# Six loads in two transfers each, in a prefix log-sum-exp on one core

## The chip, the cores and the metric

The kernel runs on one core of one Trainium2 chip. The metric is the device time in microseconds (us), smaller is better; it is given as the median of several runs. A profile of one execution stands beside it: its span runs from the first to the last instruction of that execution.

## What is computed

The input x has the shape (4, 4096, 4128): four batches, 4096 time steps, 4128 columns, all float32. The output is the running log-sum-exp along the time steps:

```python
out[:, 0, :] = x[:, 0, :]
for t in range(1, S):
    mx = np.maximum(out[:, t - 1, :], x[:, t, :])
    out[:, t, :] = mx + np.log(np.exp(out[:, t - 1, :] - mx) + np.exp(x[:, t, :] - mx))
```

So out[t] is the logarithm of the sum of exp(x) over all steps up to t. Input and output have 270.5 MB each.

## The kernel before, in words

**Tiles.** The kernel takes exp of all values, forms running sums and takes their logarithm. One step of the kernel handles 128 x r consecutive time steps of one batch, with r = 2 or 3: partition p of the tile (a row of SBUF, the on-chip memory) holds r neighbouring time steps of 4128 columns each. A load or a store of such a tile is one transfer of 128 rows with 16,512 bytes times r per row: 33,024 bytes for r = 2 (4,128 KB in all) and 49,536 bytes for r = 3 (6,192 KB). The lists `begin`, `usual` and `final` (L149 to L151) give r for each step of a batch; the first batch starts with 2, 2, 2, 3, 2, 3. There are 49 steps, 49 loads and 49 stores.

**Slots.** Four slots in SBUF hold the tiles in turn (x0 to x3; L71 and L72). A load may go into a slot once the store of the step four before it is done.

**One step.** Each tile is cut into three chunks of 1376 columns. For each chunk ScalarE (ACT) takes exp in place (L102); VectorE (DVE) adds up the r time steps of a partition (L114, L116) into a vector z; TensorE (PE) multiplies z by a triangular matrix (L124), which gives each partition the sum of all partitions before it and the carry of the step before; VectorE adds that to the tile (L133) and forms the last time step's sum in z (L141, or L136 in a batch's last step); ScalarE takes the logarithms (L146, L147).

**Order.** The order on each engine is written out by hand in lists (L166 to L205), and a loop (L220 to L233) emits the operations once their inputs have been emitted. All transfers are issued by SyncE (SP) on one queue. The list `moves` (L166 to L175) sets their order: loads 0 to 3, store 0, store 1, load 4, store 2, load 5, store 3, load 6 and so on. SP takes this list in order: a store waits on SP for the logarithms of its step, and a load waits on SP for the store that frees its slot, with everything after them held back.

**Completion.** Each transfer counts up one of eight semaphores, which the framework gives out in turn. At the kernel's end SP waits for each of these in turn, and a check on the inputs' range (L236 to L256) decides whether a slow general routine must run; it does not for this input.

The change is in `Step.load` (L87 and L88), which issues one transfer for a tile, and ahead of `begin` (L149).

Of the kernel before, what the change touches and what calls it, by code (L numbers as in the profile page):

```python
# [12 lines left out]
P = 128  # L13
# [8 lines left out]
def kernel(  # L22
# [5 lines left out]
    nc = tc.nc  # L28
# [17 lines left out]
        out=below, in_=below, pattern=[[1, P]], compare_op=ALU.is_ge,  # L46
# [5 lines left out]
        out=carried, in_=below, pattern=[[0, P]], compare_op=ALU.not_equal,  # L52
# [25 lines left out]
    class Step:  # L78
# [6 lines left out]
            return rows.rearrange("(p j) d -> p j d", j=self.r)  # L85

        def load(self):  # L87
            nc.sync.dma_start(out=self.xt, in_=self.dram(x))  # L88

        def store(self):  # L90
            nc.sync.dma_start(out=self.dram(out), in_=self.xt)  # L91
# [1 line left out]
    class Chunk:  # L93
# [49 lines left out]
        def log(self):  # L143
            t, r = self.t, self.t.r
            e = t.xt[:, 0:r - 1, self.cols]
            nc.scalar.activation(e, e, ACT.Ln)  # L146
            nc.scalar.activation(t.xt[:, r - 1, self.cols], self.z, ACT.Ln)  # L147

    begin = [2, 2, 2, 3, 2, 3, 2, 3, 2, 3, 3, 3, 2]  # L149
    usual = [3, 2, 3, 2, 3, 3, 3, 2, 3, 3, 3, 2]  # L150
# [70 lines left out]
    while any(at[e] < len(l) for e, l in lists.items()):  # L221
# [17 lines left out]
        out=fits[:, :B * NC], in0=probe, scalar1=LARGE, scalar2=None, op0=ALU.is_le,  # L239
    )  # L240
    nc.vector.tensor_scalar(
        out=fits[0:1, B * NC:], in0=short, scalar1=0.0, scalar2=None, op0=ALU.is_le,
# [7 lines left out]
        out=flag, in0=good, scalar1=float(P), scalar2=None, op0=ALU.is_lt,  # L250
# [62 lines left out]
```

## Time and profile before

| | before |
|---|---|
| median of 3 runs | 1260.83 us (1260.6 to 1261.09) |
| span of the profiled execution | 1258.4 us |
| DVE busy | 956.2 us (76%), 548 instructions |
| ACT busy | 955.4 us (76%), 466 instructions |
| PE busy | 602.4 us (48%), 884 instructions |
| moved by DMA | 541.28 MB, mean 430 GB/s |
| packets of all transfers of the kernel (queue q1) | 14,112, of which 1,568 of 4 bytes |
| load of 6,192 KB: issue to landing | 38.4 us median, 30 of them |
| load of 4,128 KB | 33.0 us median, 19 of them |
| store of 6,192 KB and of 4,128 KB | 25.0 us and 21.6 us median |

The profile gives no time of the execution other than its span; the median of the timed runs is 2.4 us longer. How to read it: the page has a busy share for each engine, then 40 equal slices of the span with a digit for each engine (tenths busy) and the rate of the DMA in GB/s. "DMA share" is the mean busy share of the core's 16 DMA engines, which together work off what SP puts on its queue. A table by stage gives the same for stretches of time that the reader chooses: length, then for each engine busy time and (in brackets) instructions, then the granted TensorE clock, the DMA share and the GB/s. SPq is SP's issuing of transfers. Single records of the trace hold a start and a length for each row of a transfer and for the 4-byte records that end a transfer, 16 for each.

### The profile page before, as it was taken

To read this page: it belongs to the slowest core of one execution; us is meant where nothing else is said; L and a number is where in the kernel's file an instruction comes from. 1 tells how busy PE (TensorE), PEld (TensorE's weight loads), DVE (VectorE), ACT (ScalarE), POOL (GpSimd) and SP (SyncE) were. 2 spreads that over 40 slices of the span, in tenths; PEclk is the share of its full clock that TensorE was granted. 3 is DMA by queue.
4 is the path that set the end of the run, shared out by engine and by line. 5 is a ranking of instruction groups with operands and counts; after the bars stand their busy time and mean duration, and the time that the engine had idled before them with its cause. 6 is when DMAs were issued, how large, how long until landed. Compare 5 with 4: busy or idle time off the path is not lost.

```text
span 1258.4 us, 3228 instructions
## 1 busy us (share of the span) xinstructions
PE 602.4 (48%) x884; PEld 233.1 (19%) x884; DVE 956.2 (76%) x548; ACT 955.4 (76%) x466; POOL 4.6 (0%) x14
## 2 busy tenths in 40 slices
PE   3654454453535455345364535634535553463361
PEld 1221121121212122112121212211211211121120
DVE  3997696795967699579596679957957976795792
ACT  6987687786976699578697668866968966896792
POOL 1000000000000000000000000000000000000000
PEclk9877776676677667666676666766766776676676
DMA  9999999999999999999999999999999999999998
GB/s 403 420 439 426 432 436 428 432 437 429 439 425 438 430 437 433 436 435 427 440 422 436 436 432 434 434 430 435 437 428 437 431 435 431 434 437 433 432 435 354
DMA packets 14131, 541.28 MB, mean 430 GB/s; under 512 B 1568, under 2 KB 1568, under 8 KB 1568
## 3 DMA queue, kind: packets, MB, share of 16 engines
q1 hardware_dynamic: 14112, 541.07, 99.6%
q8 instruction: 7, 0.11, 0.0%
q14 instruction: 12, 0.10, 0.0%
HBM read 270.53 MB, written 270.53 MB: 430 GB/s over the span
## 4 chain that ended last, share of the span: by engine, by line
DMA 69%; ACT 14%; DVE 13%; PE 1%; issue 1%; SPq 0%; ACTq 0%; DVEq 0%
DMA x<-in_x_dram 52%; DMA out_dram<-x 17%; ACT x L102 6%; DVE x L133 5%; ACT x L146 5%; DVE z L116 3%; ACT x L147 3%; DVE z L141 3%; DVE x L114 2%; PE p L124 1%; SPq L91 0%; DVE z L136 0%; ACTq L146 0%; ACTq L254 0%; SPq L88 0%
## 5 line engine op out<-in xcount | busy, mean ns | idle before, releaser
L124 PE MATMUL p<-z,carried 128*128 128x512 f32 (+1 forms) x810 | 551.8, 842 | 544.3 <-DVE z L116 544.3
L102 ACT ACTIVATE x<-x 128x4128 f32<-128x4128 f32 (+1 forms) x147 | 468.0, 3187 | 219.7 <-DMA x<-in_x_dram 219.7
L124 PEld LDWEIGHTS p<-z,carried 128*128 128x128 f32 x810 | 213.4, 280 | 882.2 <-DVE z L116 648.3
L133 DVE TENSOR_TENSOR x<-p,x 128x2752 f32<-128x2752 f32 (+1 forms) x147 | 361.9, 2462 | 6.2 <-PE p L124 6.2
L146 ACT ACTIVATE x<-x 128x2752 f32<-128x2752 f32 (+1 forms) x147 | 300.6, 2045 | 63.5 <-DVE z L141 58.5
L114 DVE TENSOR_TENSOR x<-x 128x1376 f32<-128x1376 f32 x90 | 142.9, 1588 | 216.5 <-ACT x L102 216.5
L116 DVE TENSOR_TENSOR z<-x 127x1376 f32<-127x1376 f32 x147 | 233.9, 1591 | 53.8 <-ACT x L102 49.4
L141 DVE TENSOR_TENSOR z<-x 128x1376 f32<-128x1376 f32 x135 | 215.0, 1592 | 4.6
L147 ACT ACTIVATE x<-z 128x1376 f32<-128x1376 f32 x147 | 196.0, 1334 | 0.0
L124 PE MATMUL p<-z,below 128*128 128x512 f32 (+1 forms) x72 | 50.4, 864 | 87.4 <-DVE z L116 87.4
L124 PEld LDWEIGHTS p<-z,below 128*128 128x128 f32 x72 | 19.6, 289 | 117.7 <-DVE z L116 78.8
L136 DVE CUSTOM_DVE_ANT_0 z<-x 128x1376 f32<-128x1376 f32 x12 | 19.1, 1592 | 0.4
L105 ACT ACTIVATE spare<-x,tiny 1x1376 f32<-1x1376 f32 x12 | 17.3, 1442 | 0.5
L69 POOL MEMSET z<- 128x1376 f32 x3 | 3.7, 1241 | 0.0
L105 ACT ACTIVATION_READ_ACCUMULATOR spare<-x,tiny 1x1 f32 x12 | 2.2, 186 | 0.0
L247 PE MATMUL good<-ones,low 128*1 128x1 f32 x2 | 0.2, 164 | 3.8 <-DVE low L245 3.8
L34 ACT ACT_TABLE_LOAD x1 | 1.3, 1283 | 0.8 <-PEq L297 0.8
L136 DVE DVE_READ_ACCUMULATOR2_ANT probe<- 128x1 f32 x12 | 1.0, 83 | 0.0
L247 PEld LDWEIGHTS good<-ones,low 128*1 128x1 f32 x2 | 0.1, 80 | 4.8 <-DVE low L245 4.8
L249 DVE TENSOR_SCALAR flag<-good 1x1 int32<-1x1 f32 x1 | 0.1, 148 | 0.3 <-PE good L247 0.3
L51 POOL TENSOR_SCALAR_AFFINE_SELECT carried<-below 128x128 f32<-128x128 f32 x1 | 0.3, 290 | 0.0
L45 POOL TENSOR_SCALAR_AFFINE_SELECT below<-below 128x128 f32<-128x128 f32 x1 | 0.3, 285 | 0.0
(13 smaller groups left out, 1.6 us busy)
## 6 DMA issues: line engine op xcount, KB each, us to landing
x<-in_x_dram SPq DMA_DIRECT2D x30, 6192.0 KB, 38.4
out_dram<-x SPq DMA_DIRECT2D x30, 6192.0 KB, 25.0
x<-in_x_dram SPq DMA_DIRECT2D x19, 4128.0 KB, 33.0
out_dram<-x SPq DMA_DIRECT2D x19, 4128.0 KB, 21.6
```

The lines of the kernel that those rows point to most:

```text
L34: nc.scalar.preload_act_table_set("natural_log_exp_and_others")
L69: nc.gpsimd.memset(t, 0.0)
L102: nc.scalar.activation(e, e, ACT.Exp)
L105: nc.scalar.activation(spare, t.xt[0:1, 0, self.cols], ACT.Relu, bias=tiny, scale=-1.0, accum_out=short[:, k:k + 1],)
L114: nc.vector.tensor_tensor(out=e[1], in0=e[0], in1=e[1], op=ALU.add)
L116: nc.vector.tensor_tensor(out=self.z[0:n], in0=e[r - 2][0:n], in1=e[r - 1][0:n], op=ALU.add,)
L124: nc.tensor.matmul(pt[:, a:b], lhsT=w, rhs=self.z[:, a:b], start=True, stop=True,)
L133: nc.vector.tensor_tensor(out=e, in0=base, in1=e, op=ALU.add)
L136: nc.vector.tensor_tensor_reduce(out=self.z, in0=ends[0], in1=ends[1], scale=1.0, scalar=0.0, op0=ALU.add, op1=ALU.add, accum_out=probe[:, ...
L141: nc.vector.tensor_tensor(out=self.z, in0=ends[0], in1=ends[1], op=ALU.add)
L146: nc.scalar.activation(e, e, ACT.Ln)
L147: nc.scalar.activation(t.xt[:, r - 1, self.cols], self.z, ACT.Ln)
```

## The change

`load` issues one transfer for each part of a list of partition ranges, and the list has two entries for steps 0 to 5 and one for all others. Step 0 goes out as partitions 0 to 15 and 16 to 127, steps 1 to 5 as partitions 0 to 63 and 64 to 127. Both parts stand one behind the other on SP. The run then has 104 transfers in place of 98.

```diff
         def load(self):
-            nc.sync.dma_start(out=self.xt, in_=self.dram(x))
+            for a, b in parts.get(self.n, [(0, P)]):
+                nc.sync.dma_start(out=self.xt[a:b], in_=self.dram(x)[a:b])
...
+    parts = {0: [(0, 16), (16, P)]}
+    parts.update((k, [(0, P // 2), (P // 2, P)]) for k in range(1, 6))
+
     begin = [2, 2, 2, 3, 2, 3, 2, 3, 2, 3, 3, 3, 2]
```

## The prediction

> **What bounds the kernel now.** I read the slices of the page first, then the DMA queues, then the table by stage, and only then the engines.
>
> ```profile
> DVE  3997696795967699579596679957957976795792
> ACT  6987687786976699578697668866968966896792
> ...
> DMA  9999999999999999999999999999999999999998
> GB/s 403 420 439 426 432 436 428 432 437 429 439 425 438 430 437 433 436 435 427 440 422 436 436 432 434 434 430 435 437 428 437 431 435 431 434 437 433 432 435 354
> ```
> ```profile
> q1 hardware_dynamic: 14112, 541.07, 99.6%
> ```
>
> See that no engine is at its limit for long, while the 16 DMA engines are busy in every slice and move 420 to 440 GB/s in every slice but the first and the last. 541.07 MB at 433 GB/s is 1250 us of a span of 1258.4. So the end is set by the DMA queue's own work, all of it on one queue (q1, issued by SP), and a microsecond lost there is lost at the end: no compute wait can give it back. The trace's records agree: summed over the 16 engines, they are idle for only 5.8 us of the span, 2.1 of it at the start, 3.1 at the end (the engines run dry between 1251 and 1257 us), and 0.6 in all the rest.
>
> The second question is what sets the pace of a busy DMA engine. This is the table by stage, with the DMA share and GB/s as its last columns:
>
> ```profile
> 15.00:20.00 5.00, 2.60 (x3) 1.17 (x4) 1.90 (x2) 4.87 (x5) 0.00 (x0) 1.00 1.01 436
> 20.00:25.00 5.00, 4.62 (x10) 1.99 (x8) 3.90 (x3) 4.97 (x5) 0.00 (x0) 1.00 1.01 436
> ...
> 1245.00:1250.00 5.00, 0.00 (x0) 0.00 (x0) 0.00 (x0) 0.00 (x0) 0.00 (x0) 0.50 1.01 436
> 1250.00:1255.00 5.00, 0.00 (x0) 0.00 (x0) 0.00 (x0) 0.00 (x0) 0.00 (x0) 0.50 0.56 239
> ```
>
> At 15 to 25 us only loads are in flight; at 1245 to 1255 only stores. Both run at 436 GB/s. And when half of the engines have run dry (share 0.56), the rate falls in proportion: 239 / 0.56 = 427. The engines that are left do not get faster, so the pace is no shared total; it is private to each of the 16 paths. Single records say the same: a row of 33,024 bytes takes 1.222 us in all but 3% of 4,864 cases, one of 49,536 bytes 1.829 us, both 27 GB/s, 1/16 of 436. Private to what, though: to the DMA engine, or to the group of SBUF rows at its other end? In this kernel every transfer has all 128 rows, so that the two are never seen apart. The change pulls them apart, and everything hangs on that.
>
> **The change, part by part.** It changes `load` (L87-L88) for steps 0 to 5. Six transfers are added; no byte, no compute instruction, no order of loads and stores on SP.
>
> 1. Issue. In the profile the first four loads are issued back to back from 0.80 us:
>
> ```profile
> 0.80 1.91 SPq L88 DMA_DIRECT2D x<-in_x_dram  x4
> 38.04 15.04 SPq L91 DMA_DIRECT2D out_dram<-x  x2
> 58.05 0.34 SPq L88 DMA_DIRECT2D x<-in_x_dram  x1
> 70.28 0.33 SPq L91 DMA_DIRECT2D out_dram<-x  x1
> ```
>
> An issue costs 0.34 to 0.54 us of SP (L88, 49 of them). Six more are some 2.4 us of SP, four beside the 46 us in which the queue works off the first four loads, two (steps 4, 5) while the store ahead of them is moving. What is queued behind the added issues is the next store, and SP waits 973 us for ACT in front of its stores. Cost 0; without that cover it would be 0.4 us each.
>
> 2. Completion records. The page has 1,568 packets under 512 B: 98 transfers x 16. Now 104 x 16. Six more per engine at 9 ns each (the trace's length of one): 0.05 us.
>
> 3. Start. The first load is issued at 0.80 and the 16 engines start their first row between 1.81 and 2.63 us. A transfer of 16 rows, one per engine, may start them sooner. Not shown by any row; bounds 0 and -1.0 us (nothing starts before its issue). It must then have its second part issued before the first rows end, at 3.65 us: two issues end by 1.9, so it has. I take -0.4.
>
> 4. End. Completions go round eight semaphores. With 98 = 12 x 8 + 2 transfers the last store has the second; after it lands SP looks at the other six, from 1257.15 to 1257.56 us. With 104 = 13 x 8 it has the eighth, so that these looks are done before it lands: -0.4 us.
>
> 5. Waits. The exp of steps 0 to 5 (L102) waits for two parts in place of one, and so starts with the later; the parts are in one queue, so that is when the whole load landed before. The second half of load 5 also waits for a semaphore that the first half of load 3 used: long landed. Nothing is behind it but store 3. 0.
>
> 6. The pace of a part. Loads 1 to 5 carry 2+2+3+2+3 = 12 rows of 16,512 B per partition: 12 x 128 x 16,512 = 25.4 MB, 58.2 us at 436 GB/s. If the pace is the engine's own, parts of 64 rows take as long as before: 0. If it belongs to groups of SBUF rows, 64 rows reach half of the groups, two engines share each, and a row takes 2.44 us in place of 1.222: +58.2 us. These are the two ends, and they are far apart. A row of the trace that decides does not exist; I take the upper end, on a lean: the pace is private, the same in both directions and steady to a nanosecond, as that of a fixed link would be, and I see no reason why the 16 links at the SBUF should each be wider than the 16 engines that the kernel already keeps at 99.6%. The halves do not make up for each other, since the queue is worked off in order: all engines have first-half rows, then all have second-half rows. They overlap only by as much as the engines are out of step (0.8 us at the start): I take -2 us for the five loads.
>
> [...]
>
> Load 0 likewise: its 16 rows (1.2 us) may share a quarter of the groups, +3.7 us, or none; its 112 rows (8.5 us) reach both halves, 0 to +8.5, of which I take 2.
>
> Sum: 58.2 - 2 + 3.7 + 2 + 0.05 - 0.4 - 0.4 = **+61 us**. Span 1258.4 + 61 = 1319.5; the median of the runs shown, 1260.83, is 2.4 us over the span of the profiled execution, and I carry that over: **1322 us**. Its own range: 1300 (engines drift far enough out of step that a third of the loss is hidden) to 1332 (no overlap, and load 0 at its upper ends: 58 + 12).
>
> **Rivals.**
>
> *The pace is the engine's own* (or rows have fixed engines, so that a first half keeps eight engines busy and the second half the other eight, side by side). Then items 2 to 4 are all there is: 0.05 - 0.4 - 0.4, about 1260.0, from 1259.0 (start at its bound) to 1261.5 (a completion per part held up somewhere). For it: the equal rate of loads and stores could as well be the engine's. Against it: nothing but the lean above. It ends on the other side of my forecast, and its deciding point is plain: a row of a half load takes 1.222 us, not 2.4. 0.33.
>
> *Finer sharing.* If an engine's rows are dealt in turn (rows 0 to 15 first, one per engine), sixteen neighbouring rows reach only a quarter of the groups and four engines share one: up to 3 x 58 = +175 us, less as engines fall out of step; 1350 to 1435. Against it: it needs two things unseen. 0.07.
>
> *Faster by more than 2.5 us.* The first switch from loads to a store, near 44.5 us, stretches the row in hand on all 16 engines by 0.6 to 1.4 us, and the engines end up to 5.6 us apart. Parts of 64 could put them out of step so that both shrink: the mean of the ends is 3.1 us before the last, so up to that; 1257. 0.06, since nothing orders it so.
>
> *That the change does nothing* is within the first: the built program does issue 104 transfers, of 16, 112 and ten times 64 rows.
>
> **How the numbers follow.** Forecast 0.54, engine's pace 0.33, finer 0.07, faster 0.06. 0.2% is 2.5 us, about what a measurement of this kernel can tell from no change. Faster 0.06; within it 0.33; slower 0.54 + 0.07 = 0.61. The range takes in the forecast with its bounds and the first rival: 1259 to 1332, which leaves out the finer sharing, the faster case and the edges.
>
> **What would show it.** In the profile after: GB/s near 220 in slices 0 to 3 wherever a half load moves, with the DMA share still 1.0; the fourth load landing near 88 us and not 46; from the sixth load on, rows at 1.829 us again; everything later shifted by one constant. If the slices stand at 403 to 439 as now, item 6 is wrong and the first rival holds. If the first rows start at 1.8 us still, item 3 is wrong; if SP still looks at six semaphores after the last landing, item 4. I am wrong in size if half-load rows take between 1.3 and 2.3 us.

## The result, and the profile after

The changed kernel takes 1330.94 us (median of 5 runs, 1330.39 to 1331.30), the kernel before 1261.09 us (5 runs, 1260.60 to 1261.29): 69.9 us more, a ratio of 1.0554 (95% interval 1.0543 to 1.0566). The forecast was 1322 us in a range of 1259 to 1332. The profiled execution took 1330.94 us itself and has a span of 1329.2 us.

The slices of the page after, and the counts of packets:

```profile
DMA  9999999999999999999999999999999999999998
GB/s 218 212 252 300 267 394 435 433 425 440 430 430 432 438 432 433 430 437 433 430 437 427 433 440 434 428 440 425 435 440 429 436 431 434 431 433 437 427 435 355
DMA packets 14227, 541.28 MB, mean 407 GB/s; under 512 B 1664, under 2 KB 1664, under 8 KB 1664
```

The DMA engines are as busy as before in every slice, but in the first six slices (some 200 us) they move 212 to 394 GB/s. From the seventh on the row reads as before. So the engines did not wait for work; the same work took longer. The table by stage (DMA share and GB/s last) shows the two speeds side by side:

```profile
30.00:35.00 5.00, 4.94 (x10) 2.12 (x8) 3.88 (x3) 4.90 (x5) 0.00 (x0) 1.00 1.00 211
50.00:60.00 10.00, 6.78 (x14) 2.87 (x13) 9.52 (x7) 7.71 (x6) 0.00 (x0) 0.84 1.02 211
100.00:110.00 10.00, 7.37 (x12) 2.91 (x12) 9.90 (x7) 8.99 (x4) 0.00 (x0) 0.77 1.01 436
120.00:130.00 10.00, 0.00 (x0) 0.00 (x0) 0.00 (x0) 0.00 (x0) 0.00 (x0) 0.59 1.01 211
```

From 30 to 60 us halves of loads are in flight, at 211 GB/s with the engines fully busy; from 100 to 110 us whole stores are, at 436, and from 120 to 130 us the halves of load 4, again at 211. The trace's landings put the loss in its places. A half of a load with two time steps per partition takes 10.1 us, where the whole took 9.8. With three time steps a half takes 15.3 us on the mean, where the whole took 15.7 (load 3) and 16.6 (load 5).

| | before, us from landing to landing | after | difference |
|---|---|---|---|
| load 0 (its last part lands at) | 13.05 | 22.81 | +9.8 |
| loads 1 to 3 | 35.2 | 70.3 | +35.1 |
| load 4 | 9.7 | 19.9 | +10.2 |
| load 5 | 16.6 | 31.0 | +14.4 |

Together +69.5, which is nearly the whole loss of 69.9. The issues on SP, for comparison with those of before:

```profile
0.80 4.68 SPq L89 DMA_DIRECT2D x<-in_x_dram  x8
52.87 20.57 SPq L92 DMA_DIRECT2D out_dram<-x  x2
102.86 1.12 SPq L89 DMA_DIRECT2D x<-in_x_dram  x2
```

Eight issues now take until 5.48 us, and the queue has work until 93 us: they cost nothing.

### The profile page after: what moved, and what is told of

It reads as the page before. It is cut to its first block, busy times and chain, and to the rows that moved or that the text cites. A ratio compares the mean times of both kernels' runs of the same rounds, so it can differ in the third digit from the quotient of the medians.

```text
span 1329.2 us, 3243 instructions
## 1 busy us (share of the span) xinstructions
PE 609.2 (46%) x884; PEld 236.9 (18%) x884; DVE 956.1 (72%) x548; ACT 955.6 (72%) x466; POOL 4.6 (0%) x14
## 4 chain that ended last, share of the span: by engine, by line
DMA 67%; ACT 13%; DVE 13%; another core or an unknown queue 4%; issue 1%; PE 0%; SPq 0%; ACTq 0%
DMA x<-in_x_dram 51%; DMA out_dram<-x 16%; ACT x L103 6%; DVE x L134 5%; ACT x L147 4%; DVE z L117 3%; ACT x L148 3%; DVE z L142 3%; DVE x L115 1%; PE p L125 0%; DVE z L137 0%; SPq L92 0%; SPq L89 0%; ACTq L147 0%
## 5 line engine op out<-in xcount | busy, mean ns | idle before, releaser
L125 PE MATMUL p<-z,carried 128*128 128x512 f32 (+1 forms) x810 | 557.8, 849 | 599.1 <-DVE z L117 599.1
L125 PEld LDWEIGHTS p<-z,carried 128*128 128x128 f32 x810 | 216.7, 285 | 941.1 <-DVE z L117 702.0
```

The source lines that it names most:

```text
L125: nc.tensor.matmul(pt[:, a:b], lhsT=w, rhs=self.z[:, a:b], start=True, stop=True,)
```

## The experiments

The theory behind the forecast: a transfer is slow when its SBUF rows reach only some of the paths that it supposes there, one for each of the 16 DMA engines of the page, so that several engines share one. The records name neither a path nor the engine of a row, so the paths and their number stay a model that no run shows; what the experiments can show is which rows are slow together. The main rivals: the number or size of the transfers, the DRAM side, and the order in the queue. Each kernel was timed beside the kernel before on the same chip (1260.7 to 1260.9 us in all groups). The diffs are against the kernel before, or against the changed kernel's list `parts`; from experiment 4 on, the lines of that list that go are left out, since they are the two shown for 2 and 3.

**1. Six loads in two parts of 128 rows each.**

```diff
-            nc.sync.dma_start(out=self.xt, in_=self.dram(x))
+            for a, b in [(0, 1), (1, self.r)] if self.n < 6 else [(0, self.r)]:
+                nc.sync.dma_start(out=self.xt[:, a:b], in_=self.dram(x)[:, a:b])
```

Expected:

> The first six loads go out as two transfers each, 104 in all, but cut along the time steps of a partition: each part has all 128 rows, with 1 and 1 or 1 and 2 of the 2 or 3 time steps. Theory (rows): a part is slow because of which SBUF rows it reaches, not because it is a part; with all 128 rows nothing is lost, and the end keeps the 0.4 us that the last store's semaphore saves: 1260.5 to 1261. Rival (count): each added transfer, or each transfer under 4 MB, costs some 10 us by itself: 1331 as in the changed kernel.

Measured: 1260.72 us beside 1260.81, ratio 0.9999 (0.9990 to 1.0008). Its table by stage over the same loads:

```profile
14.00:24.00 10.00, 6.67 (x12) 3.11 (x12) 5.07 (x4) 9.84 (x8) 0.00 (x0) 1.00 1.00 429
24.00:34.00 10.00, 4.94 (x11) 2.04 (x10) 9.52 (x7) 9.71 (x8) 0.00 (x0) 0.90 1.02 438
```

The same 104 transfers, parts as small as the halves (2,064 KB), and the full rate. Count and size are out for the halves; the first load's part of 516 KB has no counterpart here.

**2 and 3. The two pieces of the change alone.**

```diff
-    parts = {0: [(0, 16), (16, P)]}
-    parts.update((k, [(0, P // 2), (P // 2, P)]) for k in range(1, 6))
+    parts = {0: [(0, 16), (16, P)]}                                  # 2
+    parts = {k: [(0, P // 2), (P // 2, P)] for k in range(1, 6)}     # 3
```

Expected of the first load alone, then of the halves alone:

> Only the first load is cut, as 16 and 112 rows. The changed kernel's landings give 9.8 us more for this load (22.8 in place of 13.05 us). Theory (rows): the time lost at the start is not won back, 1270 to 1271.5. Rival (cover): later work hides part of it, under 1268; rival (start): the small first transfer makes the engines start sooner, and the loss belongs to the halves behind it, 1260 to 1261.

> Only loads 1 to 5 are cut in halves of 64 rows. Theory (rows): the landings of the changed kernel give 35.2 + 10.2 + 14.4 = 59.8 us for them, so 1320 to 1322, and e2 and e3 add up to the changed kernel. Rival (interaction): the loss of the halves depends on how the first load put the engines in or out of step; then the two do not add up, by more than 3 us.

Measured: 1268.74 us (1.0064, 1.0048 to 1.0079) and 1321.93 us (1.0483, 1.0467 to 1.0499), so +7.9 and +61.1. They add up to 69.0; the change costs 69.9. There is no interaction to speak of. The halves are where the theory had them. The first load alone is not: 1268.74 lies between the theory's 1270 and the 1268 below which the rival of cover was to be. Its table by stage, while the part of 112 rows moves and then while load 1 does:

```profile
7.00:22.00 15.00, 0.00 (x0) 0.00 (x0) 0.00 (x0) 0.00 (x0) 0.00 (x0) 1.00 0.94 247
22.00:32.00 10.00, 5.09 (x8) 2.39 (x9) 3.43 (x3) 9.29 (x7) 0.00 (x0) 1.00 1.00 433
```

Its landing was late by 9.5 us (22.5 in place of 13.05), but that is the last of 16 counts, which came from 12.52 to 13.05 us in the kernel before; on the mean of the 16 engines it was late by 8.7 us. One more microsecond comes back from the landing of load 2 to that of load 3, with the switch to the first store: 15.7 us pass there in the kernel before and 14.6 here. Rows were stretched by 0.6 to 1.4 us there on all 16 engines at once in the kernel before; here no row is, by more than 0.04 us. That engines which are less in step do not stretch each other's rows is a reading that no run tests.

**4. Halves that lie across the middle.**

```diff
+    parts = {k: [(0, 32), (32, 96), (96, P)] for k in range(1, 6)}
```

Expected:

> Loads 1 to 5 go out as rows 0 to 31, 32 to 95, 96 to 127: 10 added transfers in place of 5. Theory (rows, two sides): rows 0 to 63 have one half of the paths and 64 to 127 the other, and 32 rows of a side reach as many as 64; then the middle part of 64 rows reaches both sides and runs at the full 1.22 us a row (33,024 bytes), and only the outer 2 x 32 rows at 2.6: half the loss, +30, 1290 to 1292. Rival (row count): a part of 64 rows is slow wherever it lies: the middle costs as much as a half, at least +60, 1320 or more. Rival (count of transfers): twice the added transfers, +120, 1380.

Measured: 1294.13 us, +33.3 (1.0263, 1.0248 to 1.0279). Its table by stage, cut near the landings of the three parts of load 1:

```profile
13.00:18.00 5.00, 0.00 (x0) 0.00 (x0) 1.55 (x1) 4.04 (x4) 0.00 (x0) 1.00 0.89 211
18.00:23.00 5.00, 4.81 (x7) 2.29 (x8) 1.63 (x2) 4.97 (x4) 0.00 (x0) 1.00 1.15 416
23.00:28.00 5.00, 3.03 (x8) 1.23 (x6) 4.82 (x4) 4.46 (x5) 0.00 (x0) 1.00 0.96 205
```

Rows 0 to 31 at 211 GB/s, rows 32 to 95 at 416, rows 96 to 127 at 205. The middle part has 64 rows as well, and is fast: 416 GB/s beside the 211 of the halves. What counts here is not how many rows a part has but which. The time is 2 us above the expected 1290 to 1292. Half of the loss of experiment 3 is 30.6; on the mean of the 16 engines load 5 lands 31.8 us later than before, and the last store 31.9. The last engine's landing there is 34.3 us later: the engines are 7.4 us apart at the end, in place of 5.6. So most of what exceeds half is spread among the engines late in the run; what causes it is not shown.

**5. Quarters of 32 rows.**

```diff
+    parts = {k: [(s, s + 32) for s in range(0, P, 32)] for k in range(1, 6)}
```

Expected:

> Loads 1 to 5 go out as four parts of 32 rows each, 15 added transfers in place of 5. Theory (rows, two sides): rows 0 to 31 reach as many paths as rows 0 to 63, so a row takes the same 2.6 us (33,024 bytes) and the loss is that of the halves: +61, 1320 to 1324. Rival (pace goes with the number of rows of a part): a quarter of the pace, +175, 1435. Rival (count): three times the added transfers of the halves, +183.

Measured: 1322.93 us, +62.2 (1.0489, 1.0472 to 1.0507). The first two lines below are of the halves alone (experiment 3), the next two of the quarters:

```profile
24.00:34.00 10.00, 4.08 (x11) 1.53 (x9) 6.75 (x5) 4.44 (x6) 0.00 (x0) 0.98 1.01 211
34.00:44.00 10.00, 5.99 (x8) 2.49 (x9) 7.27 (x5) 10.00 (x7) 0.00 (x0) 0.51 1.01 211
```
```profile
24.00:34.00 10.00, 4.11 (x11) 1.55 (x9) 6.81 (x5) 4.33 (x5) 0.00 (x0) 0.98 1.02 211
34.00:44.00 10.00, 5.55 (x7) 2.35 (x8) 6.84 (x5) 9.73 (x6) 0.00 (x0) 0.51 1.02 211
```

32 rows run at the rate of 64 (211 GB/s in both), and 15 added transfers cost 62.2 us where 5 cost 61.1, a difference within the intervals.

**6. Parts of 16 rows.**

```diff
+    parts = {k: [(s, s + 16) for s in range(0, P, 16)] for k in range(1, 6)}
```

Expected:

> Loads 1 to 5 go out as eight parts of 16 rows each, one row per engine and part. The first load's 16 rows took 4.9 us in place of 1.22 in the changed kernel, as if four engines shared a path. Theory (rows, groups of four neighbours): if the engines stay in step every part of 16 rows takes 4.9 us (7.3 us with 49,536 bytes a row), +180, 1435 to 1445; as the next 16 rows lie on other paths, engines that finish early run ahead, and the loss may fall as far as that of the halves, +60. Rival (nothing below 32 rows matters): +60 exactly, 1321.

Measured: 1413.04 us, +152.3 (1.1197, 1.1162 to 1.1232).

```profile
24.00:34.00 10.00, 5.00 (x13) 1.96 (x11) 7.78 (x5) 5.35 (x5) 0.00 (x0) 1.00 1.06 126
34.00:44.00 10.00, 0.00 (x0) 0.00 (x0) 0.00 (x0) 0.00 (x0) 0.00 (x0) 0.52 1.08 129
```

Lower again, 126 and 129 GB/s where parts of 32 rows have 211. (The 4.9 us that the expectation gives for the first load's 16 rows is too high: in the changed kernel they took 3.26 to 4.00 us, 3.65 on the mean, where the first rows of the kernel before took 1.87.) A part lands every 4.41 us, 16 x 33,024 bytes at 120 GB/s, 3.6 times as long as a row alone and not 4 times: the loss lies between the two ends that were given, near the one for engines in step.

**7. The DRAM side.**

```diff
-            nc.sync.dma_start(out=self.xt, in_=self.dram(x))
+            if not 1 <= self.n < 6:
+                nc.sync.dma_start(out=self.xt, in_=self.dram(x))
+                return
+            nc.sync.dma_start(out=self.xt[0:64], in_=self.dram(x)[32:96])
+            nc.sync.dma_start(out=self.xt[64:P], in_=self.dram(x)[0:P:2])
```

Expected:

> Loads 1 to 5 go to SBUF in halves of 64 rows as in the change, but neither half reads one half of the tile's DRAM region: the first reads its rows 32 to 95, the second every other row of the whole region. This changes what is computed: rows of these five tiles are mixed up. Theory (SBUF rows): only the destination counts, +61, 1320 to 1323. Rival (DRAM side): 64 neighbouring rows of DRAM are what shares a path; then the second half runs at full pace and the first at that of a middle part, and the loss is gone or halved, 1261 to 1291.

Measured: 1322.27 us, +61.6 (1.0489, 1.0472 to 1.0507), and the rate of the halves (its table by stage below). Neither of these two sources makes a difference (+61.6 beside the +61.1 of experiment 3); with the same destination in SBUF comes the same loss.

```profile
24.00:34.00 10.00, 3.80 (x10) 1.44 (x8) 6.73 (x5) 4.40 (x5) 0.00 (x0) 0.94 1.02 211
```

**8. Two queues.**

```diff
-            nc.sync.dma_start(out=self.xt, in_=self.dram(x))
+            if not 1 <= self.n < 4:
+                nc.sync.dma_start(out=self.xt, in_=self.dram(x))
+                return
+            nc.sync.dma_start(out=self.xt[0:64], in_=self.dram(x)[0:64])
+            nc.scalar.dma_start(out=self.xt[64:P], in_=self.dram(x)[64:P])
```

Expected:

> Loads 1 to 3 are cut in halves of 64 rows; the first half of each is issued by SP and the second by ScalarE, on a queue of its own, at the start of the kernel. On one queue these three cost 35.2 us in the changed kernel. Theory (rows, order): the halves lose only because every engine is in the same half at the same time; with two queues an engine has rows of both halves to choose from, and those that fall out of step by one row are in different halves, so that part of the loss goes: +5 to +25, 1266 to 1286. Rival (the order makes no difference): +35, 1295 to 1297.

Measured: 1296.02 us, +35.3 (1.0279, 1.0262 to 1.0297): the rival, to the microsecond. The DMA queues, and two stretches of the table by stage:

```profile
q1 hardware_dynamic: 13920, 533.67, 97.0%
q10 hardware_dynamic: 240, 7.40, 2.6%
```
```profile
10.00:20.00 10.00, 0.00 (x0) 0.00 (x0) 0.00 (x0) 0.00 (x0) 0.00 (x0) 1.00 1.05 264
30.00:40.00 10.00, 7.40 (x12) 3.28 (x12) 5.73 (x4) 9.84 (x9) 0.00 (x0) 1.00 0.98 218
```

Both queues were served. The records show how. From 6 to 60 us rows of the two queues take turns: 16 rows of the one start (32 where a queue goes on to its next load), then as many of the other. Until 23 us SP's rows are those of load 0, which is whole, and the rate is 264 GB/s; from 28 us on the two queues hold opposite halves, and it is 218. So the rows that start together still belong to one half.

**9. Stores in halves.**

```diff
+            for a, b in [(0, P // 2), (P // 2, P)] if 1 <= self.n < 6 else [(0, P)]:
+                nc.sync.dma_start(out=self.dram(out)[a:b], in_=self.xt[a:b])
```

Expected:

> All loads whole; stores 1 to 5 go out as halves of 64 rows, 12 rows of 16,512 bytes per partition in all, as many as in loads 1 to 5. Theory (rows, both directions): the path at the SBUF rows is as narrow for reading as for writing, +61, 1320 to 1323. Rival (writing only): reads of SBUF are not held up by which rows they come from, 1260 to 1262.

Measured: 1304.91 us, +44.0 (1.0364, 1.0328 to 1.0399), with runs from 1301.5 to 1311.5. Neither number. Reading by half is slow too:

```profile
58.00:68.00 10.00, 6.53 (x10) 2.71 (x9) 8.51 (x7) 9.54 (x5) 0.00 (x0) 0.67 1.05 241
78.00:88.00 10.00, 4.96 (x6) 1.85 (x6) 5.24 (x3) 1.83 (x3) 0.00 (x0) 0.67 1.00 416
```

(halves of store 1, then a whole load). But the loss shrinks while the engines drift apart. On the mean of the 16 engines it is 7.7, 5.6 and 3.1 us in stores 1, 2 and 4, which have two time steps per partition, and 9.6 and 7.5 us in stores 3 and 5, which have three. Between the first and the last engine's landing lie 0.3 us in the first half store and 12.9 us in the last. Why they drift here, and not with halves of loads, the runs do not show.

**10. All five loads as 16 and 112 rows.**

```diff
+    parts = {k: [(0, 16), (16, P)] for k in range(1, 6)}
```

Expected:

> Loads 1 to 5 go out as 16 and 112 rows, as only the first load does in the change. For the first load that cost 9.5 us at its landing, more than the 3.7 + 2 of the forecast. Theory A (the 112 rows themselves are slow, about 1.8 times, since an engine's seven rows no longer match one group of paths): 3.2 + 6.7 us for 33,024-byte rows, half more for 49,536: 5 loads together +59, 1316 to 1322. Theory B (neighbouring rows in blocks of seven, sharing a path only where two engines happen to meet): 3.2 + 2.4 to 3.6 us, together +34 to +41, 1294 to 1302. Theory C (the first load paid for the start of the run): under +34.

Measured: 1317.24 us, +56.4 (1.0445, 1.0428 to 1.0463): the time of theory A. A cut that looks harmless, with 112 of 128 rows in one transfer, costs nearly as much as halves (+61.1). The reason that theory A gives is not shown: which rows an engine gets when it has seven (112 over 16) stands in no run; that it would be seven neighbours, with a shared path here and there (theory B), does not fit the size (1294 to 1302 was expected of it).

**11. Halves in the middle of the run.**

```diff
+    parts = {k: [(0, P // 2), (P // 2, P)] for k in (26, 27, 28, 29, 32)}
```

Expected:

> The halves of 64 rows are moved to the middle of the run, to loads 26, 27, 28, 29 and 32, which carry the same 12 rows of 16,512 bytes per partition as loads 1 to 5. There the 16 engines are 4.6 us out of step (first to last landing of a transfer in the kernel before), in place of 0.5 to 1 us at the start. A half lasts 10 to 15 us, so at its ends some engines are in the other half for up to 4.6 us. Theory (in step: the loss is there only while all engines are in the same half): between +33 and +52, 1294 to 1313. Rival (a row of a half load is slow whatever the others do): +61, 1321 to 1323.

Measured: 1320.59 us, +59.8 (1.0474, 1.0457 to 1.0492): just under the rival's 1321 to 1323, and far above the theory's 1313. In its table by stage the halves of load 29 still crawl:

```profile
740.00:760.00 20.00, 7.48 (x12) 2.86 (x12) 7.67 (x5) 7.09 (x5) 0.00 (x0) 0.64 0.95 201
```

The engines were out of step by 4 us when the first of these loads began (landings from 632.6 to 636.6 us just before). By load 29 two engines were 6 us ahead of the next, while the other 14 kept their 4 us and stayed slow. An engine that runs ahead of its fellows gains nothing for a run that ends with the slowest.

None of these versions is faster than the kernel before. Among the cuts of all loads 1 to 5, the two that cost least are the one along the time steps, which costs nothing, and the one across the middle.

## Why the prediction was right, point by point

**What bounds the kernel**: right. The loss at the landings of six loads (69.5 us) is the loss at the end (69.9), with nothing won back over 1,150 us; the DMA share stays at the top in all slices. (The 5.8 us of idle time is the mean of one engine, not a sum over 16: the first rows start at 2.06 us on the mean.)

**Items 1, 2 and 5** (issues, records, waits; nothing or 0.05): right within a microsecond; experiment 1 has all three and stands at 0.9999 (0.9990 to 1.0008).

**Item 3** (start, -0.4): the first rows start at 1.83 to 2.16 us in place of 1.81 to 2.63, on the mean 0.1 us sooner, and then last 3.65 us in place of 1.87. By the prediction's own sign (first rows at 1.8 us still) the item was wrong; it is worth nothing.

**Item 4** (end, -0.4): right as far as a trace shows it. From the end of the last row to the end of the span pass 1.75 us before and 1.35 after; 1.34 with 104 transfers in experiment 1, 1.35 with 103 and 1.66 with 99. In the time of experiment 1 it does not stand out.

**Item 6, the choice between the ends**: the upper end was the right one, and the runs show this of it: the pace goes by which SBUF rows move together (experiments 4 to 6: 416 GB/s for rows 32 to 95, 211 for rows 0 to 31, 126 for parts of 16), not by the engines' own pace (a row takes 2.59 us in a half, 1.222 in a whole load), the number of transfers (0.9999 in 1, +62.2 beside +61.1 in 5) or the place of the rows in DRAM (+61.6 in 7). That engines share links there is the author's model. The lean that led to it was an argument, not a reading; no row that the prediction shows could have told it, and the 16 links at the SBUF of which it speaks are shown by no run.

**Item 6, its size**: +56 for the halves was low, 61.1 was measured. Two reasons. The halves do not run at half the pace but at a little less: a row of 33,024 bytes takes 2.59 us in most records, not 2.44, and 211 GB/s is less than half of 436. And the -2 us for engines out of step did not come: out of step by 4 us (experiment 11) the loss is still 59.8, so that there was next to nothing to take off for 0.8. The fourth load landed at 93.1 us where 88 was expected.

**Load 0**: +5.7 was forecast; 9.5 to 9.8 at its landing and 7.9 at the end were measured. Both of its terms were mis-sized, and the groups of rows that they were taken from are shown by no run. The 16 rows took 3.65 us on the mean in place of 1.87, +1.8 where 3.7 was forecast (later in a run, where rows of the kernel before take 1.22 and those of experiment 6 take 4.4, it would be +3.2). The 112 rows are the larger miss: 2 was chosen between 0 and 8.5, and 6.7 came, 15.2 us for what should take 8.5.

**The sum**: the two pieces as measured give 61.1 + 7.9 = 69.0, beside 69.9 for the change and 61 in the forecast. The time is 1.1 us under the top of the range, and that it stays under it is in part luck: the halves cost 61.1, more than the 58.2 that the prediction took for their upper end, and load 0 cost 7.9, less than its upper ends of 12.2.

**The rivals**: the engine's own pace falls with the first profile after. Finer sharing was rightly given little: rows of the halves take 2.59 us, where rows of parts of 16 take 4.4 (experiment 6), and the 64 rows of the middle run at 416 GB/s (experiment 4). With parts of 16 rows the pace does fall further, by a factor of 1.7 and not the 2 of that rival. Of the faster case one part exists: with the first load cut the stretch at the first switch is gone (experiment 2: 0.04 us at the most in place of 0.6 to 1.4), worth 1 us beside a loss of 69.9.

## What to carry to other kernels

Where the DMA is the bound, look at which SBUF rows a transfer reaches before it is cut: a cut along the free dimension cost nothing here (a ratio of 0.9999), while a cut along the partitions took all parts but the middle one of experiment 4 to about half the rate or less (198 to 264 GB/s, 109 to 129 with parts of 16 rows), and a second queue for the halves did not help (+35.3 beside +35.1). The busy share of the DMA hides this: here it was 1.00 at 211 GB/s and 1.01 at 436. Read the GB/s beside it. And a gain of tenths of a microsecond (a semaphore's place, a start) must first be priced against the pace of the bytes that it moves about.

## What the runs showed of the hardware that was not expected

- 112 rows in one transfer run at 0.56 of the full pace (8.55 / 15.2 us); how rows are dealt to the engines then stays open.
- Two queues that hold opposite halves are served in turn, 16 rows of the one and then 16 of the other: no gain (+35.3 beside +35.1).
- Halves of stores cost less than halves of loads (+44 beside +61) and put the engines up to 12.9 us out of step; with halves of loads 14 of the 16 stay within 4 us (experiment 11). Why is open.
- A row of 33,024 bytes moves at 27 GB/s in a whole load (1.222 us), at 12.8 in a half (2.59 us) and at 7.5 in a part of 16 rows (4.41 us). From halves to sixteens it loses a factor of 1.7, where the theory would have 2. That is not explained.
